# The planner of TensorE's order in the attention: a capped guess at a short wait becomes a look at what runs on the engine

## Chip, cores and metric

The kernel runs on one core of one Trainium2 chip. The metric is the device time of one execution in microseconds (us). The kernel before takes 1211.18 us, the median of three runs (1210.94 to 1211.78).

## The reference

One decoder layer for 1024 tokens of width 1024, in float32. What matters here is the first half:

```python
h = _rmsnorm(x, g_mix)
proj = h @ w_in                      # q, k, v of two groups of heads
# (a) stick-breaking attention, 8 heads of 64, in blocks of 128 queries
z = q @ k.T * SCALE
log_survive = cumsum(log_keep, reverse=True) - log_keep
weights = where(strict, exp(log_beta + log_survive), 0)
o_sb = weights @ v
# (b) differential attention with ALiBi, 4 heads of two maps each
z = q @ k.T * SCALE - slope * dist
attn = softmax(z1) - lam * softmax(z2)
o_df = attn @ v
x = x + concat(rmsnorm(o_sb), rmsnorm(o_df)) @ w_out
```

After it come a mixture of 16 experts (two for each token), a gated per-layer input and a last RMSNorm. The change does not touch them.

## The kernel before, in words

**The attention** works through eight pairs of heads: pairs 0 to 3 are stick-breaking (two heads of 64 each), pairs 4 to 7 differential (one head with two maps). While one pair is attended, the keys, queries and values of the next are projected, so TensorE has two streams to choose from. Its steps are:

- **S** (`scores`, lines 355 to 365): the scores of 128 queries against up to 512 keys. In a stick-breaking row ScalarE makes two sigmoids of them (lines 404 and 405), VectorE one scan over the whole row (line 408) and GpSimd one product (line 409). In a differential row VectorE adds the distances (line 432), ScalarE exponentiates (439), and the two maps are scaled and joined (448, 450).
- **T** (`turn_rows`, lines 368 to 390): four (on the diagonal three) transposes of 128 x 128 turn two finished rows into a PSUM tile `tp`; `split` (lines 53 to 55) then makes a rounded copy `wth` on ScalarE and from it the remainder `wtl` on VectorE. Two PSUM buffers exist for it. These splits are issued at a higher priority.
- **V** (`value`, lines 475 to 504): the product with the values. It needs `wth` (line 488) and `wtl` (line 489) of its group, and its result is taken out of one PSUM buffer by lines 499 or 503 and 504.
- **F** (`finish_o`): the output goes to memory, its squares are summed.
- **P** (`group_items`, lines 211 to 234): one item is two 128-row slices of a projection, six matmuls of 512 columns (lines 228 to 230); four items make a group, and its result is taken out by the functions `evac_k`, `evac_q` and `evac_v`. A *weights* item loads and splits the next weights (lines 195 and 201).

**The order on TensorE** is written out ahead of time, when the program is built, by the class `Mix` (from line 535). It keeps a clock `pe` for TensorE and, for ScalarE, VectorE and GpSimd, a time `at` at which the work given so far would be done. Each step has a fixed cost on TensorE (0.44 for a T, 0.47 or 0.7 for a V, some 1.365 for a P item; all in us, all written in the code), and books costs on the other engines by `on(engine, ready, duration, first)`. Ordinary work begins when its engine's queue is done. Work with `first=True`, the splits and evacuations that are issued at a higher priority, is taken to begin when it is ready or when the queue is done, but at most 0.7 us after it is ready:

```python
start = max(self.at[eng], ready)
self.at[eng] = start + dur
return (min(start, ready + 0.7) if first else start) + dur
```

Four of the times that the planner keeps come out of such calls: when a V may go (`wready`, line 618: ScalarE 0.6, VectorE 0.7, then 0.15), when a T finds a free PSUM buffer (`tpfree`), when the next pair of rows may use the output's buffer (`pvfree`), and when the next projection group finds one (`mmfree`). A weights item books 1.1 on ScalarE from 4.0 after its issue and 1.25 on VectorE behind that, without `first`.

At each step `run` takes the first of V, T, S, F that is ready by its clock. A ready P item goes instead if there is none, or if the projections' share of the work done is behind the attention's. If nothing is ready, the clock is put forward to the earliest. The chosen step is issued at once, and TensorE's instructions keep that order (`manual_schedule` over TensorE alone). The other engines' instructions are ordered by the scheduler from priorities and from the order of issue; `high_priority` puts an instruction 150 places ahead.

Of the kernel before, what the change touches and what calls it, by code (L numbers as in the profile page):

```python
# [534 lines left out]
class Mix:  # L535
# [3 lines left out]
    def __init__(self, k, wt):  # L539
        self.k, self.wt = k, wt  # L540
        self.pe, self.at = 0.0, {"act": 0.0, "dve": 0.0, "pool": 0.0}
        self.S, self.T, self.V, self.F, self.P = [], [], [], [], []
        self.zfree, self.tpfree, self.pvfree, self.mmfree = [0.0] * 3, [0.0] * 2, [0.0], [0.0] * 2
        self.done, self.tot = {}, {}
        self.nT = self.nV = 0
        self.emit = lambda c, f: f()

    def on(self, eng, ready, dur, first=False):

        start = max(self.at[eng], ready)  # L550
        self.at[eng] = start + dur
        return (min(start, ready + 0.7) if first else start) + dur

    def add_pair(self, P, p, units, proj):
        main = 0.0
# [1466 lines left out]
```

## Time and profile before

| | |
|---|---|
| median of three runs | 1211.18 us |
| the profiled execution, its own time | 1211.68 us |
| its span, first to last instruction | 1209.8 us |
| mean granted TensorE clock | 0.983 |
| TensorE busy with matmuls | 1136.6 us (94%) |
| VectorE busy | 908.0 us (75%) |
| ScalarE busy | 722.5 us (60%) |
| GpSimd busy | 177.5 us (15%) |

The span is what the profile covers; the execution's own time is 1.9 us longer. In the profile PE is TensorE's matmuls, PEld its weight loads, DVE VectorE, ACT ScalarE, POOL GpSimd. The end of a matmul is modelled, so a busy PE need not be at its peak. The attention of the stick-breaking pairs lies at about 59 to 300 us of the span, that of the differential pairs at about 300 to 550 us; from about 500 us on the output projection is mixed in.

### The profile page before, as it was taken

To read this page: it belongs to the slowest core of one execution; us is meant where nothing else is said; L and a number is where in the kernel's file an instruction comes from. 1 tells how busy PE (TensorE), PEld (TensorE's weight loads), DVE (VectorE), ACT (ScalarE), POOL (GpSimd) and SP (SyncE) were. 2 spreads that over 40 slices of the span, in tenths; PEclk is the share of its full clock that TensorE was granted. 3 is DMA by queue.
4 is the path that set the end of the run, shared out by engine and by line. 5 is a ranking of instruction groups with operands and counts; after the bars stand their busy time and mean duration, and the time that the engine had idled before them with its cause. 6 is when DMAs were issued, how large, how long until landed. Compare 5 with 4: busy or idle time off the path is not lost. (4 is left out here: it accounts for less than half of the span.)

```text
span 1209.8 us, 22567 instructions
## 1 busy us (share of the span) xinstructions
PE 1136.6 (94%) x8076; PEld 825.0 (68%) x8185; DVE 908.0 (75%) x2043; ACT 722.5 (60%) x1404; POOL 177.5 (15%) x275
## 2 busy tenths in 40 slices
PE   6999999998999999889999799999999999997996
PEld 4666656665666666556555588988989989884443
DVE  8677786767767667869986677777888879765875
ACT  6576776766766575745533366666767667654442
POOL 0133333333200000000000111111121112010000
PEclk9999999999999999979999899999999999998998
DMA  6212120120222121513876688998999999938611
GB/s 211 68 31 75 31 74 27 45 61 23 62 59 64 44 67 40 183 58 130 285 242 223 217 263 275 286 342 263 330 306 283 337 279 333 291 109 314 241 73 52
DMA packets 211756, 202.53 MB, mean 167 GB/s; under 512 B 12698, under 2 KB 182682, under 8 KB 211643
## 3 DMA queue, kind: packets, MB, share of 16 engines
q1 hardware_dynamic: 205688, 180.22, 47.8%
q0 software_dynamic: 5808, 20.58, 4.6%
q8 instruction: 65, 1.06, 0.4%
q14 instruction: 49, 0.39, 0.1%
q10 hardware_dynamic: 146, 0.27, 0.1%
HBM read 163.03 MB, written 29.62 MB: 159 GB/s over the span
## 5 line engine op out<-in xcount | busy, mean ns | idle before, releaser
L228 PE MATMUL mm<-hT,whi 128*128 128x512 f32 (+1 forms) x416 | 209.5, 505 | 1.4 <-DVE Ql L264 0.9
L1629 PE MATMUL gu<-xh,mhiu 128*128 128x128 f32 (+4 forms) x512 | 155.1, 314 | 0.0
L230 PE MATMUL mm<-hT,wlo 128*128 128x512 bf16 (+1 forms) x409 | 152.0, 372 | 2.8 <-issue 0.2
L1629 PE MATMUL gu<-xh,mhig 128*128 128x128 f32 (+4 forms) x512 | 153.4, 307 | 0.0
L229 PE MATMUL mm<-hT,whi 128*128 128x512 bf16 (+1 forms) x378 | 140.9, 373 | 1.0 <-DVE hT L184 0.9
L1631 PE MATMUL gu<-xbl,mhig 128*128 128x128 bf16 (+4 forms) x512 | 124.4, 243 | 2.6 <-DVE xbl L1542 2.6
L1631 PE MATMUL gu<-xbl,mhiu 128*128 128x128 bf16 (+4 forms) x512 | 124.4, 243 | 0.0
L1632 PE MATMUL gu<-xh,mblg 128*128 128x128 bf16 (+4 forms) x512 | 119.3, 233 | 0.0
L1632 PE MATMUL gu<-xh,mblu 128*128 128x128 bf16 (+4 forms) x512 | 119.3, 233 | 0.0
L55 DVE TENSOR_TENSOR mdl<-mrawd,mdh 128x1024 bf16<-128x1024 f32 x64 | 78.2, 1222 | 44.3 <-ACT mdh L54 41.0
L54 ACT ACTIVATE wth<-tp 128x512 fp32r<-128x512 f32 (+2 forms) x168 | 70.3, 446 | 60.9 <-PE tp L378 46.2
L55 DVE TENSOR_TENSOR wtl<-tp,wth 128x512 fp32r<-128x512 f32 (+2 forms) x168 | 79.2, 493 | 36.5 <-ACT wth L54 35.1
L54 ACT ACTIVATE mdh<-mrawd 128x1024 fp32r<-128x1024 f32 x64 | 67.6, 1056 | 55.6 <-PE ya L1661 47.3
L55 DVE TENSOR_TENSOR mblg<-mrawg,mhig 128x1024 bf16<-128x1024 f32 x64 | 78.3, 1223 | 29.8 <-ACT mhig L54 29.7
L228 PEld LDWEIGHTS mm<-hT,whi 128*128 128x128 f32 x416 | 79.4, 191 | 29.4 <-PE mm L230 1.4
L409 POOL TENSOR_TENSOR row<-row,keep 128x127 f32<-128x127 f32 (+3 forms) x64 | 77.8, 1216 | 143.8 <-DVE keep L408 97.4
L229 PEld LDWEIGHTS <-whi 128*128 128x128 bf16 x416 | 40.4, 97 | 84.7 <-issue 79.6
L1629 PEld LDWEIGHTS gu<-xh,mhig 128*128 128x128 f32 x512 | 97.3, 190 | 0.6 <-ACT xh L1541 0.2
L1629 PEld LDWEIGHTS gu<-xh,mhiu 128*128 128x128 f32 x512 | 96.7, 189 | 0.0
L408 DVE TENSOR_TENSOR_SCAN keep<-keep,zx 128x128 f32<-128x128 f32 (+3 forms) x64 | 85.5, 1347 | 14.1 <-ACT keep L404 13.5
L46 POOL DMA_INDIRECT y_d<-yo,put x27 | 44.5, 1649 | 290.0 <-ACT yo L1679 185.8
L54 ACT ACTIVATE mhig<-mrawg 128x1024 fp32r<-128x1024 f32 x64 | 67.4, 1053 | 18.6 <-PE gu L1632 11.9
(351 smaller groups left out, 3266.9 us busy)
## 6 DMA issues: line engine op xcount, KB each, us to landing
mrawg<-in_w_expert_gate_dram SPq DMA_DIRECT2D x64, 512.0 KB, 5.9
mrawu<-in_w_expert_up_dram SPq DMA_DIRECT2D x64, 512.0 KB, 6.5
mrawd<-in_w_expert_down_dram SPq DMA_DIRECT2D x64, 512.0 KB, 4.5
wraw<-in_w_in_dram SPq DMA_DIRECT2D x24, 512.0 KB, 3.9
yg<-y_d SPq DMA_DIRECT2D x16, 512.0 KB, 6.2
xt<-in_x_dram SPq DMA_DIRECT2D x8, 512.0 KB, 6.7
oT_d<-ot SPq DMA_DIRECT2D x32, 128.0 KB, 2.1
wraw<-in_w_out_dram SPq DMA_DIRECT2D x8, 512.0 KB, 3.5
```

The costliest lines, as they stand in the source:

```text
L46: i = k.nc.gpsimd.indirect_dma_start(out=out, out_offset=bass.IndirectOffsetOnAxis(ap=idx, axis=0), in_=src, in_offset=None)
L54: nc.scalar.activation(hi, src, AF.Copy)
L55: (eng or nc.vector).tensor_tensor(lo, src, hi.bitcast(FT), OP.subtract)
L228: nc.tensor.matmul(ps, hi[:, c, :], hT[:, c % 4, :], start=(c == 0), stop=False)
L229: nc.tensor.matmul(ps, wv[:, c, :], k.hT[half][2][:, c, o:o + n], start=False, stop=False)
L230: nc.tensor.matmul(ps, lo[:, c, :], hv[:, c % 4, :], start=False, stop=(c == NC - 1))
L408: nc.vector.tensor_tensor_scan(a, a, k.zeros.to_broadcast([128, n]), 1.0, op0=OP.mult, op1=OP.add)
L409: nc.gpsimd.tensor_tensor(beta[:, :n - 1], beta[:, :n - 1], keep[:, 1:n], OP.mult)
L1629: nc.tensor.matmul(ps[:, x], hi[:, c], xh[:, c], start=(c == 0), stop=False)
L1631: nc.tensor.matmul(ps[:, x], hv[:, c], xl[:, c], start=False, stop=False)
L1632: nc.tensor.matmul(ps[:, x], bl[:, c], xv[:, c], start=False, stop=(c == NC - 1))
```

## The change

The planner keeps for each engine a list of the last runs that it booked (up to 13 intervals). Work with `first=True` is now taken to begin when it is ready, or, if an interval in the list covers that moment, at the end of that interval (the latest, if several do). The engine's queue time `at` is booked as before, and ordinary work begins as before. No cost, no instruction and no buffer is changed; what can change is the order of TensorE's steps, and with it the order of issue that the other engines' scheduler sees.

```diff
@@ class Mix, __init__
         self.pe, self.at = 0.0, {"act": 0.0, "dve": 0.0, "pool": 0.0}
+        self.runs = {x: [] for x in self.at}
@@ Mix.on
         start = max(self.at[eng], ready)
         self.at[eng] = start + dur
-        return (min(start, ready + 0.7) if first else start) + dur
+        if first:
+            start = max([ready] + [t1 for t0, t1 in self.runs[eng] if t0 <= ready < t1])
+        self.runs[eng] = self.runs[eng][-12:] + [(start, start + dur)]
+        return start + dur
```

## Rows read from the trace of the kernel before

**Rows 1.** The page's head and its first part: busy time, share of the span, number of instructions of each engine.
```profile
span 1209.8 us, 22567 instructions
PE 1136.6 (94%) x8076; PEld 825.0 (68%) x8185; DVE 908.0 (75%) x2043; ACT 722.5 (60%) x1404; POOL 177.5 (15%) x275
```

**Rows 2.** Busy time by stretch of the span. Columns: the stretch, its length, busy us (instructions) of PE, PEld, DVE, ACT and POOL, the granted clock, the share of the DMA engines' time, GB/s.
```profile
59.00:150.00 91.00, 88.36 (x512) 58.42 (x521) 68.88 (x106) 64.28 (x156) 33.49 (x48) 1.00 0.19 45
150.00:300.00 150.00, 138.82 (x794) 91.76 (x808) 110.65 (x147) 98.31 (x230) 54.86 (x77) 0.99 0.17 47
300.00:500.00 200.00, 194.05 (x1071) 127.38 (x1090) 140.40 (x431) 130.67 (x283) 10.38 (x34) 1.00 0.23 66
600.00:1210.00 610.00, 579.50 (x4930) 454.50 (x4984) 461.59 (x976) 343.02 (x569) 71.57 (x57) 0.98 0.78 253
```

**Rows 3.** Who waited for whom in the stick-breaking pairs, 59 to 300 us: the waiting engine, line and tile, what ended the wait; us in total, times, longest.
```profile
ACT wth L54 <- PE tp L378: 28.8, 21, 3.6
DVE wtl L55 <- ACT wth L54: 23.6, 28, 3.5
PE pv L489 <- DVE wtl L55: 7.5, 8, 1.4
PEld pv L489 <- DVE wtl L55: 6.7, 5, 1.7
PE tp L378 <- DVE wtl L55: 2.8, 1, 2.8
```

**Rows 4.** The same for PE alone in the differential pairs, 300 to 500 us (the whole answer).
```profile
PE mm L283 <- ACT vt L278: 2.3, 4, 0.7
PE z L800 <- DVE dfm L432: 2.1, 2, 1.1
PE z L800 <- DVE dfr L442: 0.2, 1, 0.2
```

**Rows 5.** PE in order of time around one turn of pair 1: start, duration, engine, line, operation, tiles, count, and in brackets the idle time before it with what ended it.
```profile
154.12 1.04 PE L378 MATMUL tp<-ident,row 128*128 128x128 f32 x8
...
158.02 0.48 PE L488 MATMUL pv<-wth,V 128*128 128x256 f32 x1
159.87 0.38 PE L489 MATMUL pv<-wtl,V 128*128 128x256 f32 x1 [1.37 <-DVE wtl L55]
```

**Rows 6.** ACT in order of time over the same turn, columns as in Rows 5.
```profile
154.36 1.05 ACT L195 ACTIVATE whi<-wraw 128x1024 fp32r<-128x1024 f32 x1
156.09 0.59 ACT L251 ACTIVATE K<-mm 64x512 fp32r<-64x512 f32 x1 [0.69 <-DVE K L252]
156.71 1.09 ACT L54 ACTIVATE wth<-tp 128x512 fp32r<-128x512 f32 x2
```

**Rows 7.** DVE in order of time over the same turn.
```profile
155.37 0.68 DVE L252 TENSOR_TENSOR K<-mm,K 64x512 fp32r<-64x512 f32 x1
156.09 0.42 DVE L504 TENSOR_TENSOR ot<-pv,ofold 64x256 f32<-64x256 f32 x1
156.43 1.93 DVE L201 TENSOR_TENSOR wlo<-wraw,whi 128x1024 bf16<-128x1024 f32 x1
158.40 0.69 DVE L252 TENSOR_TENSOR K<-mm,K 64x512 fp32r<-64x512 f32 x1
159.12 1.29 DVE L55 TENSOR_TENSOR wtl<-tp,wth 128x512 fp32r<-128x512 f32 x2
```

**Rows 8.** Groups of DVE instructions by shape, 150 to 300 us: line, operation, tiles and shapes, count; busy us, mean ns of one; idle time before them and what ended it.
```profile
L55 DVE TENSOR_TENSOR wtl<-tp,wth 128x512 fp32r<-128x512 f32 x26 | 17.1, 681 | 11.4 <-ACT wth L54 11.3
L201 DVE TENSOR_TENSOR wlo<-wraw,whi 128x1024 bf16<-128x1024 f32 x7 | 14.1, 2020 | 2.4 <-ACT whi L195 2.4
L408 DVE TENSOR_TENSOR_SCAN keep<-keep,zx 128x1024 f32<-128x1024 f32 x5 | 11.4, 2278 | 0.0
L408 DVE TENSOR_TENSOR_SCAN keep<-keep,zx 128x896 f32<-128x896 f32 x5 | 10.1, 2021 | 2.0 <-ACT keep L404 2.0
L408 DVE TENSOR_TENSOR_SCAN keep<-keep,zx 128x768 f32<-128x768 f32 x5 | 8.8, 1752 | 1.5 <-ACT keep L404 1.4 <-POOL wtl L384 0.2
L408 DVE TENSOR_TENSOR_SCAN keep<-keep,zx 128x640 f32<-128x640 f32 x4 | 5.9, 1487 | 0.3 <-ACT keep L404 0.2
```

**Rows 9.** The same, 300 to 500 us.
```profile
L55 DVE TENSOR_TENSOR wtl<-tp,wth 128x512 fp32r<-128x512 f32 x23 | 15.1, 685 | 8.3 <-ACT wth L54 8.2
L201 DVE TENSOR_TENSOR wlo<-wraw,whi 128x1024 bf16<-128x1024 f32 x9 | 11.0, 1225 | 1.0 <-ACT whi L195 0.9
```

**Rows 10.** ACT over the same stretch: the rounded half of the split.
```profile
L54 ACT ACTIVATE wth<-tp 128x512 fp32r<-128x512 f32 x23 | 12.8, 592 | 7.1 <-PE tp L378 7.0
```

**Rows 11.** One turn of a differential pair in order of time, PE and DVE, columns as in Rows 5.
```profile
381.60 1.03 PE L378 MATMUL tp<-ident,row 128*128 128x128 f32 x8
...
382.93 1.29 DVE L55 TENSOR_TENSOR wtl<-tp,wth 128x512 fp32r<-128x512 f32 x2 [1.06 <-ACT wth L54]
...
384.44 0.36 PE L488 MATMUL pv<-wth,V 128*128 128x256 f32 x1
```

## The prediction

> **What bounds the kernel now.** I read the page's busy shares first: TensorE is busy 94% of the span, no other engine over 75% [rows 1]. By stretch, the attention is the part in which that can move: from 150 to 300 us PE is busy 138.8 of 150 us, from 300 to 500 us 194.1 of 200 us [rows 2]. The 610 us behind 600 us hold none of the planner's steps, and I leave them as they are. So in the attention TensorE sets the time, it always has projection items to fill in with, and what the planner can win or lose is the time in which TensorE stands at an instruction that was put too early. The waits name it: in the stick-breaking pairs TensorE waited 7.5 us in 8 places for the remainder `wtl` ahead of a V, and once 2.8 us for a `tp` buffer ahead of a T [rows 3]; the weight loads ahead of the same V's waited 6.7 us, mostly the same time seen on the other queue. In the differential pairs no V waits at all [rows 4]. These are the waits that `wready` and `tpfree` are meant to foresee; the rest (`vt`, the sums of F) the change does not estimate, since those steps carry no readiness from a split.
>
> **One turn, followed.** The transposes of 154.12 end at 155.16; the V that needs them begins at 158.02, 2.86 later, and its second matmul at 159.87, after a wait [rows 5]. 2.85 is the largest value that the old estimate can give: 0.7 + 0.6 on ScalarE, 0.7 + 0.7 on VectorE, 0.15. So here both caps applied, and both were too small: ScalarE had the weights (until 155.41) and a key evacuation ahead of `wth`, VectorE a row of four instructions (0.68, 0.42, 1.93, 0.69 us) ahead of `wtl`, which ends at 160.41, 5.25 us after the turn [rows 6, 7]. The new rule sees one instruction on each engine: the rest of the weights, 0.25, and the rest of what DVE does at about 156.0, between 0.05 and 0.5. It gives 155.16 + 0.25 + 0.6 + (0.05 to 0.5) + 0.7 + 0.15 = 156.9 to 157.4, so V is asked for 0.6 to 1.1 us earlier than now, where now is already too early. The reason is general: a queue of several is not seen by a rule that looks at the one running.
>
> **The change part by part.** (1) The list itself costs the chip nothing; it exists when the program is built. No instruction or DMA is added, removed or resized.
>
> (2) The estimate of a split. Walking the planner's costs along the order of the kernel before, the old waits are 0.46 on ScalarE and 0.59 on VectorE, mean of the 80 turns of the stick-breaking pairs, and 0.63 and 0.60 of the 40 differential turns: the cap of 0.7 decides in well over half of them, because the queue time `at` is nearly always ahead (a weights item alone pushes it 5 us ahead). The same walk with the running interval in place of the cap gives 0.20 and 0.38, and 0.16 and 0.20. So V's, and T's that need a buffer, are asked for earlier by 1.05 - 0.58 = 0.47 us in the first half, and by 1.23 - 0.36 = 0.87 us in the second. The trace supports the size: for a moment taken at random the rest of the running instruction is the sum of count x duration squared over twice the stretch. On DVE the six groups shown give (26 x 0.681² + 7 x 2.02² + 5 x 2.278² + 5 x 2.021² + 5 x 1.752² + 4 x 1.487²) / 300 = 0.37 [rows 8]; on ACT, busy 98.3 us with 230 instructions, at least 0.655 x 0.427 / 2 = 0.14 [rows 2]. That is 0.51 or a little more, beside caps of 1.4.
>
> (3) What it costs. **Stick-breaking pairs:** the 8 V's that wait now would each wait 0.47 longer, 3.8 us. V's that now begin less than 0.47 after their split begin to wait; I count as many again at half the shift, 1.9 us. **Differential pairs:** no V waits now, since the old estimate was generous: a turn that ends at 382.63 has its `wtl` at 384.22, 1.59 later, and the V begins at 384.44, 0.22 behind it [rows 11]. The shortest value of the new estimate is 0.6 + 0.7 + 0.15 = 1.45 (the split itself takes 0.59 and 0.69 [rows 9, 10]), 0.14 under what this good case took. With the 0.36 of the walk it is 1.81. Bounds for the 40 turns: nothing, if another item stands between anyway, and 40 x (0.87 - 0.22) = 26 us, if all V's moved by the whole shift; I take the end near the row, a quarter of the turns by 0.34 us, 3.4 us. Together 9.1 us. **Given back:** while a V waits, ScalarE and VectorE work off their queues, and the next split is sooner; I take half, which leaves 4.5 us. Bounds of this part: 0 and 9.1.
>
> (4) What it gains. In 16 of the 80 stick-breaking turns of the walk the running interval on VectorE is longer than the cap, up to 1.5, because a scan takes 1.49 to 2.28 us [rows 8]. There V is put later, and one P item of about 1.4 us fills in. One wait of the eight, about 1 us, goes; none of the named waits would be the lower bound, all of them (7.5 + 2.8) the upper.
>
> (5) `mmfree` and `pvfree` also come sooner, but a projection group lasts 4 x 1.365 us, more than its evacuation, and one item fills where a row's V is held: nothing, the cover being P items; if they ran out, up to the same 0.87 in each of 16 row pairs, inside the bounds above.
>
> Sum: 4.5 - 1.0 = **+3.5 us**. On the profiled execution's 1211.68 us (span 1209.8 and 1.9 around it) that is 1215.2; the median of the runs is 0.5 lower, so I predict **1214.7 us**.
>
> **The rivals.** *Faster, by the scans.* The eight waits are just those behind scans, the remembered run sees them, and V's and the one T go behind a P item. Six of the 10.3 us of named waits gone: 1205.2 us. For it: the scans are the longest high-traffic work on VectorE, and a value that follows the engine should sort the splits better than one that is nearly a constant. Against: the turn followed above, where the wait comes from a row of four. It decides if the wait of `pv` for `wtl` between 59 and 300 us falls under 4 us.
>
> *No change that can be measured.* A V goes between two items, and an item of P lasts 1.4 us, longer than the shift; the pacing by shares puts the P's back. The order changes, the sum of waits does not: 1211.2 us. For it: PE is at 97% in the second half [rows 2], and no V waits there. That the order does not change at all I rule out nearly wholly, since the values differ at most turns.
>
> *A larger loss, by the weights.* The interval of the weights' remainder is booked as 1.25, and the row shows 2.02 us mean between 150 and 300 us, where POOL is busy 54.9 us, against 1.225 us between 300 and 500 us, where POOL is busy 10.4 us in 200 [rows 2, 8, 9]. What is remembered as running is then over 0.77 too soon, 7 times in 150 us; the cap of 0.7 had covered most of that by chance. With a V behind each, 7 x 0.77 = 5.4 us more than my forecast: 1220.1 us. The Trainium skill has the rule beside this row (SBUF — State Buffer, section "Who interferes with whom"): a VectorE instruction with two SBUF inputs contends with a GpSimd instruction that reads SBUF. By that rule, the trace agrees with 2020 against 1225 ns, and it speaks against trusting a remembered length while GpSimd works.
>
> **How the numbers follow.** I give the forecast 0.34, the larger loss 0.14, no change 0.24, the faster rival 0.28. A measurement of this kernel can tell about 0.2%, 2.4 us, from no change. Forecast and larger loss are slower by more than that: 0.48. The likeliest sign's own range is 1213.6 to 1222. Faster weighs more than its argument alone, because a new order also reshuffles what the scheduler issues on ScalarE and VectorE, by amounts that no row shows and of either sign; the named waits of 10.3 us bound it below at 1201, and 9.1 + 5.4 us without return bound it above at 1225. I take 1204 to 1222, which leaves about 2 in 10 outside.
>
> **What would show it.** Right: the wait of `pv` for `wtl` grows from 7.5 us in 8 places to some 10 to 13 us in 12 or more between 59 and 300 us, a line of that kind appears between 300 and 500 us with 1 to 4 us, the stretch behind the attention keeps its length. The gap between the transposes' end and V's first matmul shrinks in the differential pairs. Wrong: these waits fall (the scans were it), or they grow and the attention ends no later (returned in full), or the stretch behind 600 us changes its length.

## The result: 0.6% slower, and the profile after

The changed kernel takes 1219.61 us, the median of four runs (1218.15 to 1222.01), against 1211.48 us for the kernel before in the same comparison: a ratio of 1.0062 with a 95% interval from 1.0050 to 1.0074, or some 7.5 us more (the two medians are 8.1 us apart). The profiled execution has a span of 1216.4 us, 6.6 us more than before. The forecast was 3.5 us more.

First the page's head and its first part, then the busy time by stretch (columns as in [rows 2]).

```profile
span 1216.4 us, 22683 instructions
PE 1145.0 (94%) x8185; PEld 827.3 (68%) x8185; DVE 908.5 (75%) x2043; ACT 722.0 (59%) x1404; POOL 178.6 (15%) x275
```
```profile
150.00:300.00 150.00, 140.49 (x811) 93.07 (x810) 110.75 (x147) 99.15 (x234) 55.97 (x79) 0.98 0.17 47
300.00:500.00 200.00, 192.57 (x1053) 124.03 (x1051) 136.31 (x420) 126.65 (x271) 11.72 (x31) 1.00 0.21 59
```

DVE, ACT and POOL do what they did, to within 1.1 us over the whole span [rows 1]; no work was added. (More PE records than before only means that fewer are missing.) What is late is the attention: VectorE and ScalarE have done 4.1 and 4.0 us less of their work between 300 and 500 us [rows 2]. The last V begins at 586.24 us where it began at 580.04, 6.2 of the 6.6 us. What follows takes as long as before. The two rows are PE in order of time, of after and of before.

```profile
586.24 0.28 PE L488 MATMUL pv<-wth,V 128*128 128x256 f32 x1
```
```profile
580.04 0.28 PE L488 MATMUL pv<-wth,V 128*128 128x256 f32 x1
```

Now PE's waits, columns as in [rows 3, 4]: first from 59 to 300 us, then from 300 to 500 us, each in full.

```profile
PE pv L489 <- DVE wtl L55: 12.5, 10, 2.1
PE pv L488 <- ACT wth L54: 1.0, 3, 0.4
PE z L804 <- POOL sums L798: 0.4, 1, 0.4
```
```profile
PE mm L283 <- ACT vt L278: 2.3, 3, 1.0
PE tp L378 <- DVE wtl L55: 1.7, 1, 1.7
PE pv L489 <- DVE wtl L55: 1.0, 2, 0.6
PE z L804 <- ACT sq L795: 0.8, 1, 0.8
PE z L804 <- POOL sums L798: 0.8, 1, 0.8
PE pv L488 <- ACT wth L54: 0.7, 1, 0.7
```

The wait of V for `wtl` grew from 7.5 us in 8 places to 12.5 us in 10, three short waits for `wth` are new, and in the differential pairs, where no V waited, three do now. The one wait of a T for a buffer (2.8 us) is gone from the first half, and one of 1.7 us is new in the second. Two turns show how it happens. This is pair 0 of the changed kernel, PE and DVE in order of time (`...` where rows are left out):

```profile
85.47 1.75 DVE L408 TENSOR_TENSOR_SCAN keep<-keep,zx 128x768 f32<-128x768 f32 x1 [0.71 <-ACT keep L404]
...
86.32 0.48 PE L488 MATMUL pv<-wth,V 128*128 128x256 f32 x1
87.14 1.26 DVE L55 TENSOR_TENSOR wtl<-tp,wth 128x512 fp32r<-128x512 f32 x2
87.86 0.38 PE L489 MATMUL pv<-wtl,V 128*128 128x256 f32 x1 [1.06 <-DVE wtl L55]
...
91.08 2.01 DVE L408 TENSOR_TENSOR_SCAN keep<-keep,zx 128x896 f32<-128x896 f32 x1
...
92.11 0.28 PE L488 MATMUL pv<-wth,V 128*128 128x256 f32 x1
93.12 0.69 DVE L252 TENSOR_TENSOR K<-mm,K 64x512 fp32r<-64x512 f32 x1
93.85 0.89 DVE L55 TENSOR_TENSOR wtl<-tp,wth 128x128 fp32r<-128x128 f32 x2
94.28 0.36 PE L489 MATMUL pv<-wtl,V 128*128 128x256 f32 x1 [1.90 <-DVE wtl L55]
```

And this the same turn before:

```profile
86.74 0.60 PE L228 MATMUL mm<-hT,whi 128*128 128x512 f32 x1
86.86 1.26 DVE L55 TENSOR_TENSOR wtl<-tp,wth 128x512 fp32r<-128x512 f32 x2
...
87.43 0.48 PE L488 MATMUL pv<-wth,V 128*128 128x256 f32 x1
87.75 0.28 PE L489 MATMUL pv<-wtl,V 128*128 128x256 f32 x1
87.87 0.28 PE L488 MATMUL pv<-wth,V 128*128 128x256 f32 x1
87.99 0.28 PE L489 MATMUL pv<-wtl,V 128*128 128x256 f32 x1
```

The remainder's split begins 0.28 us later than before (87.14 against 86.86). Before, two more slices of a projection stood in front of V, and its remainder was nearly there, so that no wait shows; after, V begins 1.11 us sooner and its second matmul stands until 87.86. The second wait, 1.90 us, is the longer kind: the scan of 2.01 us that began at 91.08 and a key evacuation stand in front of `wtl`. Where none waits, 0.32 us pass from the first matmul of a V that follows a projection to the next (87.43 to 87.75 before), and 0.12 us within the run (87.75, 87.87, 87.99). Here 1.54 us pass from 86.32 to 87.86, the start of a V, and 2.17 from 92.11 to 94.28, inside a run. So the waits were 1.22 and 2.05 us, where the brackets say 1.06 and 1.90: the modelled end of the matmul before hides some 0.15 us of each.

In the differential pairs the gap from the transposes' end to V shrank as forecast: from 1.81 us [rows 11] to 1.27 us in this turn of after (385.66 + 1.03 to 387.96), and the next V there waits. Two turns are only an example; over all of them, from the weight load of a turn's last transpose to the load of its V's first matmul, the mean went from 3.63 to 2.83 us in the 40 differential turns and from 3.62 to 3.29 us in the 80 stick-breaking ones. That is 0.80 and 0.33 us, where the forecast's walk had 0.87 and 0.47.

```profile
385.66 1.03 PE L378 MATMUL tp<-ident,row 128*128 128x128 f32 x8
...
387.96 0.48 PE L488 MATMUL pv<-wth,V 128*128 128x256 f32 x1
...
391.89 0.39 PE L489 MATMUL pv<-wtl,V 128*128 128x256 f32 x1 [0.59 <-DVE wtl L55]
```

### The profile page after: what moved, and what is told of

Read it like the earlier page. It is cut to its first block, busy times and chain, and to the rows that moved or that the text cites. A ratio compares the mean times of both kernels' runs of the same rounds, so it can differ in the third digit from the quotient of the medians.

```text
span 1216.4 us, 22683 instructions
## 1 busy us (share of the span) xinstructions
PE 1145.0 (94%) x8185; PEld 827.3 (68%) x8185; DVE 908.5 (75%) x2043; ACT 722.0 (59%) x1404; POOL 178.6 (15%) x275
## 5 line engine op out<-in xcount | busy, mean ns | idle before, releaser
L229 PE MATMUL mm<-hT,whi 128*128 128x512 bf16 (+1 forms) x416 | 156.6, 376 | 1.1 <-DVE hT L184 1.0
L230 PE MATMUL mm<-hT,wlo 128*128 128x512 bf16 (+1 forms) x416 | 155.3, 373 | 0.0
L408 DVE TENSOR_TENSOR_SCAN keep<-keep,zx 128x128 f32<-128x128 f32 (+3 forms) x64 | 85.4, 1346 | 12.4 <-ACT keep L404 11.2
L489 PE MATMUL pv<-wtl,V 128*128 128x256 f32 x240 | 67.4, 298 | 14.0 <-DVE wtl L55 13.8
```

What stands on the lines that cost most here:

```text
L229: nc.tensor.matmul(ps, wv[:, c, :], k.hT[half][2][:, c, o:o + n], start=False, stop=False)
L230: nc.tensor.matmul(ps, lo[:, c, :], hv[:, c % 4, :], start=False, stop=(c == NC - 1))
L408: nc.vector.tensor_tensor_scan(a, a, k.zeros.to_broadcast([128, n]), 1.0, op0=OP.mult, op1=OP.add)
L489: nc.tensor.matmul(po, v0, wl, start=False, stop=last and not P.df)
```

## The experiments

Twelve kernels, each timed against the kernel before. The theory is **too early**: the new estimate of a split is shorter, so V and T are put ahead of their data. Its rivals: **reshuffle** (any new order wins or loses by chance), **wrong information** (the single intervals mislead, whatever their mean), **other bookings** (the evacuations), and the **remembered length** of the weights.

### Which bookings: turns or evacuations

```diff
# the two kernels: after.py, with the new rule where first == 2, the cap elsewhere
-        if first:
+        if first == 2:
             start = max([ready] + [t1 for t0, t1 in self.runs[eng] if t0 <= ready < t1])
+        elif first:
+            start = min(start, ready + 0.7)
# turns only: the two bookings of do_t pass 2
# others only: the bookings of do_v and do_p pass 2
```

> The new rule for the two bookings of a turn alone (when a V may go, when a turn finds a buffer); output and projection evacuations keep the cap of 0.7. Theory 'too early' (V asked for ahead of its split): all of the loss is here, +0.4 to +0.8% on the kernel before, with the wait of pv for wtl over 59 to 520 us at 12 to 16 us against 7.5 before and 13.8 in the changed kernel. Rival 'reshuffle' (any new order costs or gains by chance, the estimate's size does not matter): the order differs from both kernels in many places, so anywhere between -0.5 and +0.8%, with no tie to the wait of pv. Rival 'other bookings': under +0.2%.

> The new rule for the evacuations of the outputs and projections alone; turns keep the cap. Few steps of the order move. 'Too early': within 0.2% of the kernel before, wait of pv for wtl 7 to 8.5 us. 'Other bookings': +0.4 to +0.7%. 'Reshuffle': small, since few steps move, within 0.2%.

The evacuations alone: 1.0001 (0.9992 to 1.0010). The turns alone: 1.0100 (1.0082 to 1.0117), more than the whole change and more than the 0.4 to 0.8% that were expected. "Other bookings" falls as the cause. In the turns' kernel V waits for `wtl` 10.5 us from 59 to 300 us, and from 300 to 520 us T's stand for rows that are not finished:

```profile
PE tp L378 <- DVE row L450: 10.4, 4, 3.3
PE pv L489 <- DVE wtl L55: 2.7, 2, 2.1
```

So an early V also lets the next T come early, and T's rows are estimated by the ordinary queues, which the change did not touch. Expected were 12 to 16 us of V's waits (13.2 came) but not these. They alone do not make this kernel worse than the full change: all named waits of PE from 59 to 600 us come to 30.1 us, against 29.4. What differs is the granted clock, which was lower in the stretches of these T's, as here from 420 to 440 us, where one of them waited 3.3 us; the kernel before has 1.00 there.

```profile
420.00:440.00 20.00, 16.59 (x77) 10.58 (x75) 12.45 (x34) 11.09 (x21) 0.00 (x0) 0.83 0.13 37
```

Adding up, over stretches of 20 us, the length times what the clock lacks to 1.00 gives 19.0 us from 59 to 600 us, against 10.4 in the changed kernel. Which of the evacuations' bookings keeps the T's waits away is open.

### Which pairs

```diff
# do_t of the kernel above; first half as shown, second half with 2 and 1 changed over
+        how = 1 if u.P.df else 2
-        a = self.on("act", self.pe, 0.6, True)
-        d = self.on("dve", a, 0.7, True)
+        a = self.on("act", self.pe, 0.6, how)
+        d = self.on("dve", a, 0.7, how)
```

> The new rule for the turns of the stick-breaking pairs alone. 'Too early' by the forecast's terms: 5.7 us of 9.1 before what is given back, so about two thirds of the change's loss, +0.3 to +0.5%; in the changed kernel the stick-breaking pairs ended only 0.6 us later than before (but 4.2 us later one pair earlier), so a measured +0.0 to +0.1% would say that this half gives its loss back before it ends. 'Reshuffle': no relation to the waits.

> The new rule for the turns of the differential pairs alone; up to about 326 us the order is that of the kernel before. 'Too early': a wait of pv for wth or wtl of 1 to 4 us appears between 300 and 520 us where there was none; +0.2 to +0.5%. If the changed kernel's loss in pairs 4 and 5 (5.6 us by the marks of its trace) is made by this rule there, +0.4 to +0.6%; if it was handed on from the first half, within 0.2%.

Stick-breaking pairs alone: 1.0044 (1.0030 to 1.0058), 5.3 us; differential pairs alone: 1.0028 (1.0015 to 1.0041), 3.4 us. Together 8.7, about the whole change. V's waits for `wtl` from 59 to 300 us are 12.6 us in the first kernel and 7.5 us in the second, where they stand as before; from 300 to 520 us the second has 1.1 us of them and 1.4 us of T's. The loss of the first half is not given back before its end: pair 3's end, which came only 0.6 us late in the changed kernel, misled, because V's had been put ahead of projections that were still to be done. The first kernel's loss is not all waits, however: its clock lacks 15.6 us against 10.2 before (0.56 between 520 and 540 us), while its named waits grew by 1.0 us only.

### Shorter and longer without any list

```diff
# before.py; the cap is passed by the caller
-        return (min(start, ready + 0.7) if first else start) + dur
+        return (min(start, ready + first) if first else start) + dur
# do_t, short: 0.33 and 0.19; long: 1.1 and 0.7; longer: 1.5 and 0.7 (stick-breaking, differential)
+        cap = 0.19 if u.P.df else 0.33
# do_v, do_p: first=0.7 as before
```

> The rule of the kernel before without any list, but the cap on a turn's two waits cut from 0.7 to 0.33 (stick-breaking) and 0.19 us (differential), so that the mean estimated wait of a turn is 0.59 and 0.35 us, about that of the changed kernel (0.66 and 0.43). 'Too early': the same loss as with the list, +0.4 to +1.0%, pv waits 11 us or more between 59 and 300 us. 'Wrong information': no loss beyond 0.2%, since no interval is looked at.

> The other way: the rule of the kernel before, with the cap on the waits of a stick-breaking turn raised from 0.7 to 1.1 us (mean estimated wait 1.52 us against 1.05). 'Too early' taken further: the 7.5 us of waits before are of the same kind, so they fall to 3 to 6 us and the time falls by 0.1 to 0.5%. If the kernel before is already at the balance: within 0.2%. 'Reshuffle': no tie between the waits and the time.

> The cap for the stick-breaking turns at 1.5 us, where 1.1 gave 0.9965 of the kernel before. Mean estimated wait of a turn 1.71 us, against 1.52 and 1.05. 'Too early': the waits fall further, pv for wtl to 3 to 6 us; time between 0.993 and 0.998. If 1.1 was a chance order: 0.998 to 1.005.

Short: 1.0151 (1.0138 to 1.0165), beyond the 0.4 to 1.0% expected. Without any list, a shorter mean alone costs more than the change (it is a little shorter than the changed kernel's, 0.59 and 0.35 us against 0.66 and 0.43). "Wrong information" is not needed for a loss. Long: 0.9965 (0.9953 to 0.9978), longer: 0.9960 (0.9945 to 0.9974). The two longest of PE's waits from 59 to 300 us with the short and the long cap, the longest with the longer cap:

```profile
PE pv L489 <- DVE wtl L55: 11.2, 12, 2.1
PE pv L488 <- ACT wth L54: 1.9, 2, 1.5
```
```profile
PE pv L489 <- DVE wtl L55: 6.8, 10, 1.4
PE tp L378 <- DVE wtl L55: 1.5, 1, 1.5
```
```profile
PE pv L489 <- DVE wtl L55: 5.3, 10, 1.0
```

The time follows the waits in the forecast's direction on both sides: the kernel before was itself a little too early in its first half. With the longer cap 5.0 us of V's and T's waits are gone from that half (7.5 + 2.8 to 5.3), and 0.40% is 4.8 us. With the long cap V's waits fell to 6.8 us only, not to 3 to 6 as expected. From 1.1 to 1.5 the waits fell further but the time by less than its interval.

### The list with its mean put back

```diff
# after.py, do_t; V alone
-        u.wready[g] = d + 0.15
+        u.wready[g] = d + (1.02 if u.P.df else 0.62)
# after.py, do_t; V and the free buffer
-        d = self.on("dve", a, 0.7, True)
+        d = self.on("dve", a, 0.7, True) + (0.87 if u.P.df else 0.47)
# after.py, on; the larger of the two rules
-            start = max([ready] + [...])
+            start = max([min(start, ready + 0.7)] + [...])
```

> The changed kernel, but a V is allowed later by a constant: 0.47 us in the stick-breaking pairs, 0.87 us in the differential ones, the two shifts of the forecast. 'Too early': the loss goes, within 0.3% of the kernel before, wait of pv for wtl between 59 and 300 us back to 6 to 9 us. If the running instruction is also the better information: faster than before by 0.2 to 0.5%, wait under 6 us. Rival 'wrong information' (the single intervals point at the wrong turns, the mean does not matter): the loss of 0.6% stays and the wait stays at 11 us or more.

> The changed kernel with the whole split taken to end 0.47 us (stick-breaking) or 0.87 us (differential) later, for V's and for the free buffer of the next turn, where the run before moved V's alone and got turns that waited 9.7 us for a buffer. 'Too early': both waits fall, tp for wtl to under 4 us and pv for wtl to under 6 us between 59 and 300 us, and the time falls to within 0.2% of the kernel before, or under it by up to 0.5% if the running instruction is the better information. 'Wrong information': still +0.3% or more.

> The list is kept, but a split's wait is the larger of the old capped wait and the rest of the running instruction (mean estimated wait of a turn 1.18 and 1.28 us against 1.05 and 1.23 before). 'Too early': never earlier than before at the same state, so no loss: -0.5 to +0.2%; if the scans that the list sees are what the cap missed, pv waits under 5 us and faster than before by 0.2 to 0.5%. 'Wrong information': +0.3% or more in spite of the later estimates.

V alone later: 1.0038 (1.0024 to 1.0052), not within 0.3% as expected. V's waits did fall below those of before, but T's came for buffers that the estimate still called free too early (59 to 300 us):

```profile
PE tp L378 <- DVE wtl L55: 9.7, 5, 3.1
PE pv L489 <- DVE wtl L55: 2.8, 5, 1.0
```

Both later: **0.9903 (0.9887 to 0.9920)**, 1200.78 us, the fastest kernel here and faster than the 0.5% that were expected at best; the waits from 59 to 300 us are:

```profile
PE pv L489 <- DVE wtl L55: 5.3, 7, 1.3
PE pv L488 <- DVE ot L504: 2.2, 4, 1.2
```

The larger of the two rules: 0.9929 (0.9913 to 0.9945), also more than the 0.5% expected, and this although V's wait for `wtl` from 59 to 300 us was 9.5 us, more than before and not under 5; the T's wait for a buffer is gone. So the changed rule loses by its mean, and with a constant added to it the change wins. "Wrong information" falls. That the running instruction is the *better* information is not shown by this, though. V's waits of the best kernel in this stretch sum to the 7.5 us of before; what is gone there is T's 2.8 us and the 1.6 us of others. Adding up every named wait of PE from 59 to 600 us, the kernel before has 26.2 us, the best kernel 19.3: 11.9 against 7.5 from 59 to 300 us, 4.6 against 7.0 from 300 to 500, 9.7 against 4.9 from 500 to 600. By step, 6.3 of the 6.9 us of difference are waits of F, which no booking of a turn estimates, most of it one wait of the kernel before at 511 us:

```profile
PE zx L800 <- ACT sq L791: 4.9, 1, 4.9
```

The clock is the other part. The two rows are 500 to 520 and 520 to 540 us of before, of after, and of the best kernel, columns as in [rows 2]:

```profile
500.00:520.00 20.00, 13.28 (x65) 10.73 (x64) 16.77 (x58) 14.33 (x34) 0.47 (x3) 0.83 0.47 154
520.00:540.00 20.00, 16.97 (x71) 9.89 (x73) 11.96 (x35) 6.78 (x12) 0.35 (x2) 0.75 0.10 30
```
```profile
500.00:520.00 20.00, 16.12 (x102) 12.05 (x102) 18.11 (x53) 17.01 (x42) 1.05 (x6) 1.00 0.58 202
520.00:540.00 20.00, 15.71 (x57) 10.33 (x57) 14.61 (x54) 8.46 (x15) 0.00 (x0) 0.66 0.14 49
```
```profile
500.00:520.00 20.00, 15.29 (x68) 10.12 (x67) 17.78 (x68) 13.09 (x28) 0.00 (x0) 0.79 0.42 137
520.00:540.00 20.00, 19.86 (x97) 11.41 (x99) 10.13 (x40) 5.01 (x11) 0.35 (x2) 0.95 0.27 86
```

PE is idle there, and the granted clock falls. Taking 20 us times what is missing to 1.00: before lacks 8.4 us here, after 6.8, the best kernel 5.2; from 59 to 600 us it is 10.2, 10.4 and 5.2. So 6.9 us of waits and 5.0 of clock stand beside the 10.8 us by which the best kernel's profiled span is shorter (clock that is missing while PE waits is counted in both). The larger part, 4.8 + 3.2, lies at the seam to the output projection, 4.4 + 1.8 before 300 us, and from 300 to 500 us 2.4 are lost again. Whether the list sorts the turns better than a constant, or this order came out well by chance, stays open.

### The remembered length of the weights

```diff
# once in after.py, once in before.py (the cap, no list)
-            self.on("dve", self.on("act", self.pe + 4.0, 1.1), 1.25)
+            self.on("dve", self.on("act", self.pe + 4.0, 1.1), 2.0 if self.S and not self.S[0][0].P.df else 1.25)
```

> The changed kernel, but the weights' remainder is booked on VectorE as 2.0 us, as measured, not 1.25, while stick-breaking pairs are attended. The rival of the remembered length: what the change loses behind the weights comes back, 2 to 5 us (-0.2 to -0.4% on the changed kernel, so +0.2 to +0.4% on the kernel before). If the length is a side matter: within 0.2% of the changed kernel, +0.5 to +0.8%.

> The kernel before with the weights' remainder booked as 2.0 us on VectorE in the stick-breaking pairs; no list. Only some 14 of 702 steps move. It tells where the loss of the run with 2.0 us and the list came from. If it was the later queue for ordinary work: +0.3 to +0.7% here too. If it was the list's interval or the order's chance: within 0.3%.

With the list: 1.0121 (1.0106 to 1.0136), twice the change's loss where a return was expected. With the cap: 1.0018 (1.0009 to 1.0027), V's wait for `wtl` 8.5 us. The truer length does not help, and with the list it hurts; as the cause of the change's loss the rival has nothing for it. The measured length itself stayed: 2024 ns mean from 150 to 300 us after, as 2020 before [rows 8]. In the kernel with the list V's waits are those of the changed kernel (11.1 us for `wtl` from 59 to 300 us), so they do not explain its further 0.6%. All named waits from 59 to 600 us are 35.1 us against the changed kernel's 29.4, more than half of the 9.8 us between the two spans; why this booking makes them is open.

### The runs beside each other

V + T are PE's named waits ahead of `pv` and of line 378's `tp`, in us, 59 to 300 and 300 to 520 us together. The next column has all named waits of PE from 59 to 600 us, the next what the granted clock lacks to 1.00 over these 541 us (summed over stretches of 20 us), then the span of the profiled execution.

| kernel | V + T | all waits | clock lacks | span | ratio to before |
|---|---|---|---|---|---|
| before | 10.3 | 26.2 | 10.2 | 1209.8 | 1 |
| changed | 17.2 | 29.4 | 10.4 | 1216.4 | 1.0062 |
| turns only | 24.6 | 30.1 | 19.0 | 1224.4 | 1.0100 |
| others only | 11.9 | 26.2 | 12.0 | 1210.7 | 1.0001 |
| first half | 13.8 | 27.2 | 15.6 | 1214.9 | 1.0044 |
| second half | 12.8 | 27.3 | 12.0 | 1213.8 | 1.0028 |
| short cap | 26.1 | 34.0 | 13.8 | 1226.6 | 1.0151 |
| long cap | 8.5 | 24.2 | 8.6 | 1205.2 | 0.9965 |
| longer cap | 5.9 | 22.5 | 10.4 | 1204.1 | 0.9960 |
| list, V later | 20.9 | 28.0 | 12.4 | 1213.7 | 1.0038 |
| list, both later | 12.8 | 19.3 | 5.2 | 1199.0 | 0.9903 |
| list, the larger | 14.2 | 21.5 | 5.2 | 1199.9 | 0.9929 |
| list, weights 2.0 | 18.5 | 35.1 | 12.0 | 1226.2 | 1.0121 |
| cap, weights 2.0 | 11.3 | 27.7 | 10.4 | 1211.6 | 1.0018 |

Where the estimate was only made shorter or longer, time and V's and T's waits go together. The three kernels with the list and a later estimate lie below that line: 20.9 us of waits with 1.0038, 12.8 with 0.9903, 14.2 with 0.9929. They do fit the sum of the next two columns: against before it is +4.0, -11.9 and -9.7 us, and their spans differ by +3.9, -10.8 and -9.9. Of the other ten, seven fit to within 2.2 us; the changed kernel (+3.4 of 6.6), the short cap (+11.4 of 16.8) and the weights with the list (+10.7 of 16.4) lose more than the sum names. So the time goes with all of PE's waits and the clock together, V's and T's waits being the part that the estimate aims at. Why one order has less of the rest than another, the list's worth or "reshuffle", the sum does not tell.

## Why the prediction was right, and what was off

- **The sign and the mechanism held.** The new rule makes the estimate shorter; V is asked for earlier; V's wait for `wtl` between 59 and 300 us was forecast at 10 to 13 us and came to 12.5, though in 10 places, not 12 or more. In the differential pairs 1 to 4 us were forecast, and 2.0 us came (1.3 for `wtl`, 0.7 for `wth`, to 520 us). The stretch behind kept its length.
- **The size was off by two.** +3.5 us were forecast, about 7.5 measured. What V pays came out as forecast: V's named waits grew by 8.0 us over 59 to 600 us, and the gross sum was 9.1 - 1.0 = 8.1. The term that the measured time contradicts is "given back: while a VectorE queue drains, the next split is sooner; I take half": the time is the gross sum. The halves say the same: 5.7 us gross for the stick-breaking pairs (4.7 with the scans' gain), 5.3 measured (3.6 to 7.0); 3.4 gross for the differential, 3.4 measured (1.8 to 5.0). But the rows do not settle it. Waits of F (7.2 to 4.4 us), T (3.2 to 2.1) and `vt` (3.7 to 2.3) fell, and what is named in all grew by 3.2 us only, close to the forecast's net, though F and `vt`, which the forecast left out, wait for no split. The other 3.4 of the 6.6 us stand in no named wait. The hidden 0.15 us of each wait, 31 places against 28, would make 0.5 (an estimate), and the clock from 59 to 600 us lacks as much as before (10.4 and 10.2 us). Whether nothing was given back, or the order lost 3.4 us that the forecast has no term for, is open, and the close agreement of the first half is partly luck, since most of that kernel's loss lies in the clock.
- **The gain by the scans (-1.0)** can't be told apart from the rest. The rival that wanted waits under 4 us failed on its own point: 12.5 us.
- **No change** failed: the item of 1.4 us between did not cover a shift of 0.47 us; in the turn at 86 us it is one such item, two slices, that now stands behind V and not in front of it.
- **The larger loss by the weights** stated 1220.1 us, and 1219.61 came, but that is chance: booking the measured length made it worse.
- **The other bookings at nothing** held for them alone: 1.0001. Beside the turns' bookings they are worth something, 1.0062 against 1.0100 without them, and in the direction of a gain.

## What to carry to other kernels

In an order that is fixed ahead of time, an estimate that is too early costs a wait on the engine that sets the time. A later one was no loss here as long as other work could stand between (caps of 1.1 and 1.5 us in the stick-breaking pairs; nothing later was tried). So before a rule of an estimate is replaced by a more detailed one, compare their means with what the trace measures, and put the mean back in every time derived from it (here the buffer's as well as the data's). Then look at the whole sum of waits and the clock at the seams: a new order also moves those.

## What was not expected of the hardware

The granted clock between 500 and 540 us depends on the order: 0.79 of full speed over these 40 us before, 0.83 after and 0.87 in the fastest kernel, in a stretch where PE was busy 30.3, 31.8 and 35.2 of 40 us. Low clock there is worth some 3 us between kernels that do the same work. Over the whole attention it is more: from 59 to 600 us the clock lacks between 5.2 us (both later) and 19.0 us (turns only), and with the turns alone it was below 1.00 in stretches that hold T's waits of 1.9 to 3.3 us. A wait of TensorE may thus cost more than its own length; no run here changes the clock by itself to show it.
